# A residual block with split float32 matmuls: the distance between moving and stationary addresses is spread over 16 classes of 16 bytes

## The chip, the cores and the metric

The kernel runs on one core of one Trainium2 chip. The metric is the device time of one execution in microseconds, from runs of the same kernel; a profiled execution gives the trace beside it. TensorE (PE) does the matmuls, and its weight loads appear as an engine of their own (PEld), because they overlap the matmuls. VectorE is DVE, ScalarE is ACT, GpSimd is POOL, SyncE is SP.

## The reference, cut to what matters

One layer of a residual block over 512 tokens of width 2048 with 16 learned tokens in front. Three large products with float32 weights make up nearly all of the work:

```python
proj = h @ w_in                                   # 2048 x 12368
...                                               # sparse attention -> y_a, gated recurrence -> y_b
p = jnp.einsum('btnc,ncd->btnd', y, w_branch)     # 2 branches, 1024 x 2048 each
merged = jnp.sum(g * p, axis=2)
return x + merged @ w_out                         # 2048 x 2048
```

## The kernel before, in words

**Split products.** Each float32 operand is split into a high part, rounded to the type float32r, and the low rest. A product is then three matmuls: high by high, high weight by low moving, low weight by high moving (or, in the output, the same with the roles exchanged). The helper `hi_lo` (line 409) makes a tile `wh` (ScalarE, line 106) and a tile `wl` (VectorE, line 113; for 14 early tiles a ScalarE copy and a DMA that adds). `E.mm` records every matmul, at line 96 or 98.

**Pairs.** Most of `w_in` and all of `w_out` goes through a `Pair`: a two by two block product in the seven products of a Strassen-Winograd scheme. `SEVEN` lists them with their weights (`11`, `s2`, `12`, `s3`, `s1`, `22`, `s4`; an `s` is a sum of raw weight tiles), their moving operands and the PSUM bank that gathers them (`px`, `py`, `pz`, `pw`; `po` in the output). In `run_pair` one product is 8 blocks of 128 rows, and for each block three matmuls: `wh` by the high moving tile, `wh` by the low one, `wl` by the high one, 24 in all. The moving operands have 256 columns (tokens) in most pairs and 264 in those that need the 16 extra tokens as well. In `run_out` the roles are exchanged: the weight tiles are the moving operand of 256 columns and the tokens (`mh`) the stationary one. The weights of the next products are made two or three products ahead (`split_upto`).

**Single projections and branches.** A few column blocks of `w_in` (`kind == "in"`) and all of `w_branch` (`kind == "br"`) go through `split_chunk` and plain matmuls of 512 columns (`pg`), with 128 weight columns stationary and `hH`/`hL` or `yH`/`yL` moving.

**Where things lie.** The moving tiles live in 70 slots of 528 float32 each, 2112 bytes, which is 8 x 256 + 64. So slot number s starts at 64 x (s mod 4), counted modulo 256 bytes; the code calls s mod 4 the slot's home and asks `Slots.get` for a home when it makes such a tile (it takes another home if waiting for the right one would be long by its own clock). `HOME` gives for each of the seven products the home of the moving operand and which half of the tile it uses (the second half begins 264 x 4 = 1056 bytes on, that is 32 modulo 256); `YHOME` does so for the branches. The weight tiles have 1088 columns of which 1024 are used; all of them start at the same place modulo 256 bytes. `lead` (line 288) gives the column at which the 1024 used ones begin, 0 to 63, so it chooses the place of the weights modulo 256 bytes. Successive weight blocks inside a tile are 512 or 1024 bytes apart, so the place is the same for all of them.

**What `lead` does before.** It puts the weights so that moving address less stationary address is 192 modulo 256 bytes: `DIST` for the pairs and single projections, `DPO` for the output, `DBR` for the branches, all 192. One product of the seven cannot have it throughout: `22`, which uses `pw`, has the operand `t4`, whose high part is the first half of a slot of home 3 and whose low part is the second half of the same slot. There the high part is at 192 from the weights and the low part at 224. Where one product ends and the next begins, the distance is that of the old moving tile to the new weights.

**Order of work.** The instruction order on every engine is recorded by hand: tasks for attention, recurrence and index scores are slipped in between matmuls by a clock of estimated times (`pump`). Their matmuls appear as `phl`, `phd`, `psc` and others. Neither this clock nor the choice of slots reads a tile's offset.

Of the kernel before, what the change touches and what calls it, by code (L numbers as in the profile page):

```python
# [37 lines left out]
LAT = 180.0  # L38
SAME = {"pe": 0.0, "act": 60.0, "dve": 125.0, "pool": 60.0}
MARGIN = 300.0  # L40
DIST = 192
DPO = 192
DBR = 192
HOME = {"11": (0, 0), "s2": (2, 1), "12": (1, 0), "s3": (0, 1), "s1": (2, 0), "22": (3, 0), "s4": (1, 1)}
YHOME = (3, 0)
NSLOT = 70
# [152 lines left out]
def hybrid_kernel(ctx, tc, x, meta, vecs, w_in, rows, w_branch, w_out,  # L199
# [85 lines left out]
    def slot(name, dt=F32, home=None):  # L285
        return S.get(name, dt, home)

    def lead(home, byte, turn=False):
        return (64 * home + byte + (DPO if turn else -DIST)) % 256 // 4


    X = {}
# [101 lines left out]
    def load_upto(i):  # L394
        while state["dma"] <= min(i, len(stream) - 1):
            load_chunk(stream[state["dma"]])
            state["dma"] += 1

    def split_upto(i):
        while state["split"] <= min(i, len(preps_) - 1):  # L400
            k = state["split"]
            ch = preps_[k]
            if "pair" in ch:
                prep_op(k, ch)
            else:
                split_chunk(k, ch)
            state["split"] += 1

    def hi_lo(k, src, m, o):
        h, l = (wp.tile([128, 1088], F32R, name=f"w{i}{k}", tag=f"w{i}{k % NWS}")[:, o:o + 1024] for i in "hl")  # L410
        E.act(h[:, :m], src, AF.Copy)
        if 8 <= k < 22:
            n = l[:, :m]
            E.act(n, h[:, :m].bitcast(F32), AF.Copy, scale=-1.0)
            E.dma_add(n, src.bitcast(F32R))
        else:
            (E.ptt if k < 6 else E.tt)(l[:, :m], src, h[:, :m].bitcast(F32), OP.subtract)
        return h, l

    def split_chunk(k, ch):  # L420
        load_upto(ch["i"])
        m = ch["nk"] * ch["ncols"]
        r, nk, n = ch["raw"], ch["nk"], ch["ncols"]
        ch["h"], ch["l"] = [], []
        if k < 4:
            for g in range(2):
                h, l = slot("eh", F32R), slot("el", F32R)
                w = 4 * n
                E.act(h[:, :w], r[:, w * g:w * g + w], AF.Copy)
                (E.ptt if k > 1 else E.tt)(l[:, :w], r[:, w * g:w * g + w], h[:, :w].bitcast(F32), OP.subtract)  # L430
                early.extend((h, l))
                ch["h"] += [h[:, n * i:n * i + n] for i in range(4)]
                ch["l"] += [l[:, n * i:n * i + n] for i in range(4)]
        else:
            j = ch["job"]
            o = lead(YHOME[j.n], DIST - DBR) if j.kind == "br" else lead(ch["k0"] // 8, 32)
            h, l = hi_lo(k, r[:, :m], m, o)
            ch["h"] = [h[:, n * i:n * i + n] for i in range(nk)]
            ch["l"] = [l[:, n * i:n * i + n] for i in range(nk)]
        load_upto(ch["i"] + NRAW)  # L440
# [22 lines left out]
    def prep_op(k, op):  # L463

        pr, nm = op["pair"], op["name"]
        first = pr.raw["11"]["i"]
        load_upto(first + (0 if nm == "11" else 2 if nm == "s2" else 3))
        raw = {c: ch["raw"] for c, ch in pr.raw.items() if "raw" in ch}
        if nm in raw:
            src = raw[nm]  # L470
        else:
            for f in (sum_1, sum_2, sum_3, sum_4)[:int(nm[1]) if nm != "s1" else 1]:
                f(pr)
            src = {"s1": pr.s1, "s2": pr.s2, "s3": raw["21"], "s4": raw["12"]}[nm]
        home, half = HOME[nm]
        h, l = hi_lo(k, src, 1024, lead(home, 0, True) if pr.kind == "out" else
                     lead(home, 1056 * half + 4 * (264 - pr.w)))
        w = pr.ncols
        op["h"] = [h[:, w * i:w * i + w] for i in range(pr.nk)]
        op["l"] = [l[:, w * i:w * i + w] for i in range(pr.nk)]  # L480
        used = {"s3": 2, "22": 3, "s4": 4}.get(nm)
        if used:
            load_upto(first + used - 1 + NRAW)
# [1325 lines left out]
    for n in (1, 0):  # L1809
        for p in range(8):  # L1810
            for i in range(2):
                j = p + 8 * i
# [48 lines left out]
    for half in range(2):  # L1861
        n = (272, 256)[half]
        for kt in range(KT):
            prep_next()
            for ji in range(2):
                if ji == 0:
                    c = slice(272 * half, 272 * half + n)
                    o = kb[:80, half, :n]
                else:
                    c = slice(8 + 264 * half, 264 + 264 * half)  # L1870
                    o = qb[:, 256 * half:256 * half + 256]
# [148 lines left out]
```

## Time and profile before

| | |
|---|---|
| median of 2 runs | 1467.54 us (1467.2 to 1467.88) |
| the profiled execution | 1466.14 us |
| its span, first to last instruction | 1464.4 us |
| matmuls / weight loads | 12544 / 12544 |
| weight tiles made on VectorE (`wl`) | 289 from `raw`, 102 from `sum` |
| DMA | 263.26 MB, mean 180 GB/s |

Times in the profile are microseconds, those of one instruction in a group nanoseconds. A row of a group reads: line, engine, operation, outputs and inputs by the program's names, shapes, count, then busy time and mean duration of one, then the idle time of the engine ahead of them and what ended it. `128*128 128x256` on a matmul is weights of 128 by 128 and a moving operand of 256 columns. A piece of the chain reads: start, duration, engine, tile, line, count. A row of the timeline reads: start, duration, engine, line, operation, names, shape, count; matmuls overlap there, so the time from one start to the next is shorter than a duration. A row of the stretches reads: from and to, length, then the busy time and the count of PE, PEld, DVE, ACT and POOL, then the granted clock, the share of the DMA engines and GB/s.

### The profile page before, as it was taken

To read this page: it belongs to the slowest core of one execution; us is meant where nothing else is said; L and a number is where in the kernel's file an instruction comes from. 1 tells how busy PE (TensorE), PEld (TensorE's weight loads), DVE (VectorE), ACT (ScalarE), POOL (GpSimd) and SP (SyncE) were. 2 spreads that over 40 slices of the span, in tenths; PEclk is the share of its full clock that TensorE was granted. 3 is DMA by queue.
4 is the path that set the end of the run, shared out by engine and by line. 5 is a ranking of instruction groups with operands and counts; after the bars stand their busy time and mean duration, and the time that the engine had idled before them with its cause. 6 is when DMAs were issued, how large, how long until landed. Compare 5 with 4: busy or idle time off the path is not lost.

```text
span 1464.4 us, 31517 instructions
## 1 busy us (share of the span) xinstructions
PE 1448.0 (99%) x12544; PEld 1378.0 (94%) x12544; DVE 1183.1 (81%) x2017; ACT 715.7 (49%) x1172; POOL 272.5 (19%) x346
## 2 busy tenths in 40 slices
PE   7999999999999999999999999999999999999999
PEld 6888899999999999999999999999998888889998
DVE  6699799999999988878877887888776755878775
ACT  5576644544544554444444444444467752334332
POOL 2201000002233310100001011000365310102222
PEclk9999999999999999999999999999999999999999
DMA  9266677878889986768688687768895344458873
GB/s 278 74 157 140 154 181 190 191 183 202 204 207 227 251 197 165 176 164 199 161 202 182 152 204 177 176 162 193 208 283 160 101 125 142 144 137 223 214 214 92
DMA packets 336067, 263.26 MB, mean 180 GB/s; under 512 B 32484, under 2 KB 303408, under 8 KB 335920
## 3 DMA queue, kind: packets, MB, share of 16 engines
q1 hardware_dynamic: 306160, 174.51, 41.9%
q0 software_dynamic: 24256, 80.45, 28.3%
q10 hardware_dynamic: 5504, 6.29, 1.4%
q8 instruction: 99, 1.62, 0.4%
q14 instruction: 48, 0.39, 0.1%
HBM read 170.40 MB, written 29.98 MB: 137 GB/s over the span
## 4 chain that ended last, share of the span: by engine, by line
PE 93%; DVE 3%; DMA 2%; issue 1%; ACT 1%; POOL 0%; SPq 0%; DVEq 0%; POOLq 0%; ACTq 0%
PE pg L98 20%; PE px L96 16%; PE pz L96 15%; PE py L96 15%; PE po L96 11%; PE pw L96 8%; PE psc L98 1%; PE phl L98 1%; PE pov L96 1%; PE plg L98 1%; PE pho L98 1%; DVE wl L113 1%; PE ppt L102 1%; DMA raw<-raw 1%; PE px L102 1%
## 5 line engine op out<-in xcount | busy, mean ns | idle before, releaser
L106 ACT ACTIVATE wh<-raw 128x1024 fp32r<-128x1024 f32 x305 | 323.4, 1061 | 453.5 <-PE pz L96 116.5
L113 DVE TENSOR_TENSOR wl<-raw,wh 128x1024 fp32r<-128x1024 f32 x289 | 355.1, 1229 | 97.6 <-ACT wh L106 96.7
L96 PE MATMUL px<-hH,wh 128*128 128x256 f32 (+1 forms) x688 | 194.9, 283 | 0.0
L96 PE MATMUL px<-hH,wl 128*128 128x256 f32 (+1 forms) x688 | 192.6, 280 | 0.0
L96 PE MATMUL px<-hL,wh 128*128 128x256 f32 (+1 forms) x688 | 192.4, 280 | 0.0
L106 ACT ACTIVATE wh<-sum 128x1024 fp32r<-128x1024 f32 x102 | 108.3, 1062 | 154.5 <-PE pw L96 64.0
L98 PE MATMUL pg<-yH,wh 128*128 128x512 f32 x512 | 162.9, 399 | 1.0 <-DVE pTL L113 0.9
L96 PE MATMUL po<-wh,mh 128*128 128x256 f32 x896 | 156.6, 279 | 0.0
L113 DVE TENSOR_TENSOR wl<-sum,wh 128x1024 fp32r<-128x1024 f32 x102 | 129.6, 1271 | 27.0 <-ACT wh L106 26.6
L96 PEld LDWEIGHTS po<-wh,mh 128*128 128x128 f32 x896 | 136.9, 189 | 0.0
L96 PEld LDWEIGHTS px<-hH,wh 128*128 128x128 f32 x688 | 129.6, 188 | 0.6
L96 PEld LDWEIGHTS px<-hL,wh 128*128 128x128 f32 x688 | 129.6, 188 | 0.0
L96 PEld LDWEIGHTS px<-hH,wl 128*128 128x128 f32 x688 | 129.5, 188 | 0.0
L96 PE MATMUL pw<-tT,wh 128*128 128x256 f32 (+1 forms) x688 | 126.6, 284 | 1.5 <-DVE attn L1209 1.5
L96 PE MATMUL po<-wl,mh 128*128 128x256 f32 x448 | 125.1, 279 | 0.0
L96 PE MATMUL pz<-tT,wh 128*128 128x256 f32 (+1 forms) x688 | 122.9, 280 | 0.0
L96 PE MATMUL py<-tT,wh 128*128 128x256 f32 (+1 forms) x688 | 122.4, 279 | 0.0
L98 PEld LDWEIGHTS pg<-yH,wh 128*128 128x128 f32 x512 | 93.2, 188 | 21.3 <-PE pg L98 1.3
L96 PEld LDWEIGHTS pw<-tT,wh 128*128 128x128 f32 x688 | 105.4, 188 | 2.2 <-PE pz L96 2.0
L122 POOL DMA_DIRECT2D raw<-raw x51 | 44.3, 869 | 327.6 <-DVE sum L113 293.7
L96 PEld LDWEIGHTS py<-tT,wh 128*128 128x128 f32 x688 | 104.7, 188 | 0.0
L96 PEld LDWEIGHTS pz<-tT,wh 128*128 128x128 f32 x688 | 104.5, 188 | 0.1
(316 smaller groups left out, 3770.7 us busy)
## 6 DMA issues: line engine op xcount, KB each, us to landing
raw<-in_w_in_dram SPq DMA_DIRECT2D x192, 512.0 KB, 4.7
raw<-raw POOLq DMA_DIRECT2D x51, 512.0 KB, 5.3
raw<-sum POOLq DMA_DIRECT2D x51, 512.0 KB, 5.4
raw<-in_w_branch_dram SPq DMA_DIRECT2D x32, 512.0 KB, 4.7
raw<-in_w_out_dram SPq DMA_DIRECT2D x32, 512.0 KB, 4.2
gd<-g SPq DMA_DIRECT2D x32, 256.0 KB, 5.1
g<-gd POOLq DMA_DIRECT2D x30, 256.0 KB, 3.3
wl<-raw POOLq DMA_DIRECT2D x14, 512.0 KB, 4.5
```

The lines of the kernel that those rows point to most:

```text
L96: self.nc.tensor.matmul(out, lhsT, rhs, start=start, stop=stop, skip_group_check=True)
L98: self.nc.tensor.matmul(out, lhsT, rhs, start=start, stop=stop)
L102: self.nc.tensor.transpose(out, in_, ident)
L106: self.nc.scalar.activation(out, in_, f, **kw)
L113: self.nc.vector.tensor_tensor(out, a, b, op=op)
L122: self.nc.gpsimd.dma_start(out, a, accum_op=OP.add)
```

## The change

`lead` no longer uses one distance. It counts the weight tiles of each kind (`"in"`, `"br"`, `"out"`, and the pairs by their width 256 or 264) and gives the i-th of a kind the distance 16 x (7i + 3(i // 16)) modulo 256, so that 16 successive tiles take all 16 multiples of 16 bytes, in steps of 112, and the next 16 begin 48 bytes further. `wh` and `wl` of one tile share their distance. The sign for the output is the opposite, since there the weights are what moves. Nothing else is changed; the instructions of every engine are the same and stand in the same order.

```diff
-DIST = 192
-DPO = 192
-DBR = 192
+TURN = {}
...
-    def lead(home, byte, turn=False):
-        return (64 * home + byte + (DPO if turn else -DIST)) % 256 // 4
+    def lead(home, byte, kind):
+        i = TURN[kind] = TURN.get(kind, -1) + 1
+        dist = 16 * (7 * i + 3 * (i // 16)) % 256
+        return (64 * home + byte + (dist if kind == "out" else -dist)) % 256 // 4
...
-            o = lead(YHOME[j.n], DIST - DBR) if j.kind == "br" else lead(ch["k0"] // 8, 32)
+            o = lead(YHOME[j.n], 0, "br") if j.kind == "br" else lead(ch["k0"] // 8, 32, "in")
...
-        h, l = hi_lo(k, src, 1024, lead(home, 0, True) if pr.kind == "out" else
-                     lead(home, 1056 * half + 4 * (264 - pr.w)))
+        h, l = hi_lo(k, src, 1024, lead(home, 0, "out") if pr.kind == "out" else
+                     lead(home, 1056 * half + 4 * (264 - pr.w), pr.w))
```

## The prediction

> **What bounds the kernel now.** I read the engine table of the page first, then the chain that ended last, then the granted clock.
>
> ```profile
> PE 1448.0 (99%) x12544; PEld 1378.0 (94%) x12544; DVE 1183.1 (81%) x2017; ACT 715.7 (49%) x1172; POOL 272.5 (19%) x346
> PE 93%; DVE 3%; DMA 2%; issue 1%; ACT 1%; POOL 0%; SPq 0%; DVEq 0%; POOLq 0%; ACTq 0%
> core 0: 1464.4 us, clock 0.999
> ```
>
> TensorE is busy 99% of the span and makes 93% of the chain, at an undisturbed clock. The kernel is therefore as long as its matmuls stand apart, start to start; what another engine gains or loses matters only if it starves TensorE. The duration that a row gives a matmul (277 ns and the like) overlaps its neighbours and is no price. The price is the pace: a piece of the chain divided by its matmuls.
>
> The change moves no instruction: engine by engine, both built programs have the same instructions in the same order. Only addresses inside the weight tiles differ. So the question is whether the pace depends on where the moving operand of one matmul lies against the weights that are loaded beneath it. How many matmuls are concerned, by width, is in the groups of instructions with shapes kept apart and in two pieces of the chain:
>
> ```profile
> L96 PE MATMUL px<-hH,wh 128*128 128x256 f32 x496 | 139.4, 281 | 0.0
> L96 PE MATMUL px<-hH,wh 128*128 128x264 f32 x192 | 55.6, 289 | 0.0
> L98 PE MATMUL pg<-yH,wh 128*128 128x512 f32 x512 | 162.9, 399 | 1.0 <-DVE pTL L113 0.9
> L98 PE MATMUL pg<-hH,wh 128*128 128x512 f32 x144 | 57.1, 397 | 0.0
> 1207.92 96.48 PE pg L98 x417
> 1304.40 156.41 PE po L96 x1344
> 134.91 13.98 PE pg L98 x60
> ```
>
> A pair has seven products of 24 matmuls (8 weight blocks, 3 terms), and `px` with `hH,wh` holds 16 of the 168. So 496 / 16 = 31 pairs are 256 wide (31 x 168 = 5208 matmuls) and 192 / 16 = 12 pairs are 264 wide (2016). The output has 1344 of 256. The branch has 512 x 3/2 = 768 of 512 columns, the single projections 144 x 3 = 432.
>
> **The pace today, distance 192.** Pieces of the chain in one stretch of 256-wide pairs, and two from a later one:
>
> ```profile
> 600.38 2.73 PE py L96 x24
> 605.96 2.76 PE py L96 x24
> 608.72 2.73 PE pz L96 x24
> 618.19 2.74 PE px L96 x24
> 620.93 2.74 PE py L96 x24
> 627.28 2.82 PE py L96 x24
> 630.10 2.73 PE pz L96 x24
> ...
> 721.81 2.73 PE pz L96 x24
> 724.54 2.85 PE pw L96 x24
> ```
>
> Most products run 2.73 / 24 = 113.75 ns apart; one of the same form at the same distance took 2.82 / 24 = 117.5. The product `pw` takes 2.85 / 24 = 118.8. The seven first rows average 2.75 (114.6 ns); with one `pw` in seven the mean is (6 x 2.75 + 2.85) / 7 = 2.764 us, 115.2 ns.
>
> **`pw` is the one regular exception in the code, and so my key.** Its moving operand `t4` keeps its high half at byte 192 + 32 = 224 of the 256-byte class and its low half 1056 bytes on, at 0. The weights were placed for the high half only (224 - 32 = 192). So whenever the low half streams, the distance to the weights being loaded is 0 - 32 = 224. In order of time, against `pz`, whose halves agree:
>
> ```profile
> 721.65 0.39 PE L96 MATMUL pz<-tT,wh 128*128 128x256 f32 x2
> 721.88 0.28 PE L96 MATMUL pz<-tT,wl 128*128 128x256 f32 x1
> 721.99 0.39 PE L96 MATMUL pz<-tT,wh 128*128 128x256 f32 x2
> ...
> 724.38 0.40 PE L96 MATMUL pw<-tT,wh 128*128 128x256 f32 x2
> 724.62 0.28 PE L96 MATMUL pw<-tT,wl 128*128 128x256 f32 x1
> 724.74 0.40 PE L96 MATMUL pw<-tT,wh 128*128 128x256 f32 x2
> ```
>
> From the first start of a row of two to the `wl` row are two steps: 0.24 us in `pw`, 0.23 in `pz`; the third step is 0.12 against 0.11. A third of `pw`'s steps at 224 thus raises the whole triple by (2.85 - 2.73) / 8 = 15 ns. Address distance, or something that goes with it, moves the pace by some per cent.
>
> The 264-wide pairs behave otherwise. Undisturbed pieces, `pw` with its 224 among them, and a stretch just after other matmuls broke the stream:
>
> ```profile
> 655.41 2.91 PE pz L96 x24
> 658.32 2.89 PE pw L96 x24
> ...
> 691.36 0.29 PE L96 MATMUL px<-hL,wh 128*128 128x264 f32 x1
> 691.96 0.29 PE L96 MATMUL px<-hH,wh 128*128 128x264 f32 x1
> 692.09 0.30 PE L96 MATMUL px<-hL,wh 128*128 128x264 f32 x1
> 692.22 0.29 PE L96 MATMUL px<-hH,wl 128*128 128x264 f32 x1
> 692.47 0.28 PE L96 MATMUL px<-hL,wh 128*128 128x264 f32 x1
> 694.03 0.28 PE L96 MATMUL px<-hH,wl 128*128 128x264 f32 x1
> ```
>
> Here 224 costs nothing (2.89 / 24 = 120.4 ns). After the break, nine steps take 692.47 - 691.36 = 1.11 us, 123 ns each with single ones of 130; the next thirteen take 1.56 us, 120 each. The stream drifts through worse phases of moving against loading, then locks. Other distances may well lock in such places.
>
> **The change part by part.** It removes the common distance 192 and gives the n-th tile of a kind the distance 16 x (7n + 3(n // 16)) mod 256. All 16 classes come equally often, so 15/16 of the matmuls leave 192. In the built program, the pairs' matmuls indeed spread nearly evenly over the classes.
>
> *Pairs, 256 wide.* Lower bound of the price of leaving: none, or back to 113.75 (-1.45 ns). Upper bound: `pw`'s 15 ns put wholly on the one step at 224, 113.75 + 15 = 128.75. I take `pw`'s own mean, 118.8, since the second lock at 117.5 and the mixed steps of `pw` lie near it: (118.8 - 115.2) x 15/16 = 3.4 ns, x 5208 = +17.6 us.
>
> *Pairs, 264 wide.* Between 0 (`pw` above) and 123.3 - 120.0 = 3.3 ns. I take 1.5, in the middle: x 15/16 x 2016 = +2.8 us.
>
> *Output.* It stands at 156.41 / 1344 = 116.4 ns, between the two locks already. Bounds 113.75 and 128.75; I take 118.0, between the second lock and `pw`: 1.6 x 15/16 x 1344 = +2.0 us.
>
> *512 wide.* The projections, all at 192, run 13.98 / 60 = 233.0 ns apart. The branch runs 96.48 / 417 = 231.4, and in the built program some of its moving tiles fell into slots of other classes, so that it is a mixture of 0, 64 and 192 today. Other distances are no worse here: 432 x -1.6 x 15/16 = -0.6 us, nothing for the branch.
>
> *Writers.* The same ScalarE and VectorE instructions and DMAs fill the tiles, now from any 16-byte start. I cost that at nothing. VectorE is the nearest to a bound:
>
> ```profile
> 200.00:300.00 100.00, 100.00 (x870) 100.00 (x869) 96.64 (x196) 49.34 (x61) 8.48 (x10) 1.00 0.81 191
> L113 DVE TENSOR_TENSOR wl<-raw,wh 128x1024 fp32r<-128x1024 f32 x289 | 355.1, 1229 | 97.6 <-ACT wh L106 96.7
> L113 DVE TENSOR_TENSOR wl<-sum,wh 128x1024 fp32r<-128x1024 f32 x102 | 129.6, 1271 | 27.0 <-ACT wh L106 26.6
> wl<-raw POOLq DMA_DIRECT2D x14, 512.0 KB, 4.5
> ```
>
> The two split forms differ by 42 ns; even if each of the 391 lost that, it were 16 us of VectorE's time against 3.4 us idle in its fullest 100 us, where, at 391 over 1464 us, some 27 fall (1.1 us). Slower matmuls widen this cover. Without cover it would cost up to 16 us. The 14 DMAs land after 4.5 us and are asked three products (8.2 us) ahead.
>
> Sum: 17.6 + 2.8 + 2.0 - 0.6 = +21.8 us. On the profiled execution (1466.14 us, of which the span is 1464.4) that is 1487.9; that run lies 1.4 us under the median of 1467.54, so I forecast **1489.3 us** (+1.5%).
>
> **Rivals.**
> *Distance decides nothing.* What differs is the phase in which a product happens to start: `py` at 2.73 and 2.82 at one distance speaks for it, the regular `pw` against it. Time 1467.5.
> The Trainium skill, SBUF — State Buffer, section "Who interferes with whom", gives TensorE two independent read ports, one for the moving operand and one for the weights, and says that it waits on nobody; by that rule this rival is the outcome. The trace agrees for the 264-wide `pw` (120.4 ns) and not for the 256-wide one (118.8 against 113.75).
>
> *Bad classes.* A few distances lock in the worst phase, as 224 would at 128.75. With a quarter of the classes there and the rest at 118.8 the 256-wide mean is 121.3: (121.3 - 115.2) x 15/16 x 5208 = +29.8; the 264-wide at +3.3: +6.2; the output at 121.3: +6.2; -0.6. Together +41.6, time 1509. It decides from a pair mean near 120 ns on. For it: single 130 ns steps above; and half of the classes, the odd multiples of 16 bytes, appear nowhere in these weight products today. Against it: the stream left those steps by itself.
>
> *192 is a poor place.* Everything 256 wide settles at 113.75: pairs -1.45 x 5208 = -7.6, output -2.65 x 1344 = -3.6, -0.6 for 512; time 1455.7. For it: the 512-wide rows. Against it: 118.8 in `pw`.
>
> **How the numbers follow.** Forecast 0.49 (own range 1477 to 1497), no effect 0.22, bad classes 0.25, a poor 192 0.04. The range 1466 to 1514 holds nearly all of the first two and most of the third. Two per cent, 29.4 us, is about what a measurement of this kernel can tell from no change; above 1496.9 lie the bad classes and an edge of the forecast, 0.28; faster by as much needs more than any row offers, 0.02; within, 0.70.
>
> **What would show it.** Right: same instruction counts, PE still 99%; products of 24 spread between 2.72 and 2.95 us by class rather than clustered at 2.73; `po` near 158.5 us for 1344; branch pieces unchanged. Wrong upward: products at 3.0 us and more without another matmul inside. Wrong downward: the cluster at 2.73 stays. Wrong in kind: idle time of PE behind `wl` or `wh`.

## The result, and the profile after

The changed kernel took 1484.37 us (median of 2 runs, 1483.74 to 1485.0) against 1467.54 before: the ratio is 1.0114, with a 95% interval of 1.0093 to 1.0134. The forecast was 1489.3. The profiled execution took 1485.0 us, 18.9 more than that of before.

The engine table, the chain and the clock of the changed kernel:

```profile
PE 1465.3 (99%) x12544; PEld 1395.4 (94%) x12544; DVE 1185.9 (80%) x2017; ACT 715.5 (48%) x1172; POOL 272.5 (18%) x346
PE 91%; DVE 3%; DMA 2%; issue 2%; ACT 1%; POOL 1%; DVEq 0%; ACTq 0%; POOLq 0%
core 0: 1483.2 us, clock 1.000
```

All counts are those of before, and TensorE is still busy for 99% of a longer span at full clock. VectorE has 2.8 us more, ScalarE none. So no engine became the bound; the matmuls themselves stand further apart. Pieces of the chain in the same stretch of pairs, all 256 wide:

```profile
613.82 2.88 PE py L94 x24
616.70 2.92 PE pz L94 x24
623.63 2.85 PE pz L94 x24
626.48 2.83 PE px L94 x24
629.32 2.73 PE py L94 x24
635.72 2.85 PE py L94 x24
645.13 2.84 PE pz L94 x24
```

By the order of the tiles and the addresses of the built program, these seven have the distances 96, 208, 176, 80, 192, 160 and 240. The one at 192 still takes 2.73 us; the others take 2.83 to 2.92, which is 118 to 122 ns a matmul. The output and the 512-wide pieces:

```profile
134.97 13.96 PE pg L96 x60
1224.30 96.82 PE pg L96 x417
1321.12 158.55 PE po L94 x1344
```

The output went from 156.41 to 158.55 us. The 512-wide pieces moved by less than 0.4 us each.

Where a reader wants more than pieces show, every matmul's start can be laid beside the addresses that the built program gives its operands. The time from one start to the next, grouped by kind, gives this (sums hold everything up to the next start; means leave out steps that are more than a quarter longer than the median, where other work came between):

| kind | steps | sum before, us | sum after, us | difference | mean step before, ns | after |
|---|---|---|---|---|---|---|
| pairs, 256 wide | 5208 | 609.7 | 625.1 | +15.4 | 115.3 | 118.2 |
| pairs, 264 wide | 2016 | 249.0 | 250.0 | +1.1 | 121.1 | 121.6 |
| output, 256 wide | 1343 | 156.3 | 158.4 | +2.1 | 116.4 | 118.0 |
| single projections, 512 wide | 432 | 100.9 | 100.6 | -0.4 | 233.0 | 232.2 |
| branches, 512 wide | 768 | 182.1 | 182.5 | +0.3 | 231.7 | 232.1 |

And the 256-wide pairs of the changed kernel by distance between the moving operand and the weights that are loaded during the step:

```text
distance    0    16    32    48    64    80    96   112   128   144   160   176   192   208   224   240
mean ns  119.4 118.2 117.4 117.2 118.0 118.2 119.5 119.2 118.2 119.0 117.6 118.7 114.3 119.1 118.1 118.2
```

One class stands apart, and it is the one that all tiles had before. The fifteen others lie within 2.3 ns of each other, 118.4 in the mean. The weights' own place modulo 256 bytes, without the moving operand, does not explain it: in the kernel before, the products other than `22` have their weights at 0, 96, 128, 160, 192 and 224, all at distance 192, and their steps average 113.6 to 116.7 ns place by place; in the changed kernel, weights at these same six places but at other distances give 117.2 to 118.6.

### The profile page after: what moved, and what is told of

The parts are those of the page before. It is cut to its first block, busy times and chain, and to the rows that moved or that the text cites. A ratio compares the mean times of both kernels' runs of the same rounds, so it can differ in the third digit from the quotient of the medians.

```text
span 1483.2 us, 31517 instructions
## 1 busy us (share of the span) xinstructions
PE 1465.3 (99%) x12544; PEld 1395.4 (94%) x12544; DVE 1185.9 (80%) x2017; ACT 715.5 (48%) x1172; POOL 272.5 (18%) x346
## 4 chain that ended last, share of the span: by engine, by line
PE 91%; DVE 3%; DMA 2%; issue 2%; ACT 1%; POOL 1%; DVEq 0%; ACTq 0%; POOLq 0%
PE pg L96 20%; PE px L94 15%; PE pz L94 15%; PE py L94 14%; PE po L94 11%; PE pw L94 7%; PE psc L96 1%; PE phl L96 1%; PE pov L94 1%; PE pho L96 1%; PE plg L96 1%; DVE wl L111 1%; PE ppt L100 1%; DMA raw<-sum 1%; DMA vr<-vd 1%
## 5 line engine op out<-in xcount | busy, mean ns | idle before, releaser
L104 ACT ACTIVATE wh<-raw 128x1024 fp32r<-128x1024 f32 x305 | 323.2, 1060 | 470.6 <-PE pz L94 118.5
L94 PE MATMUL pz<-tT,wh 128*128 128x256 f32 (+1 forms) x688 | 126.3, 284 | 0.0
```

Source lines behind the costliest of these rows:

```text
L94: self.nc.tensor.matmul(out, lhsT, rhs, start=start, stop=stop, skip_group_check=True)
L104: self.nc.scalar.activation(out, in_, f, **kw)
```

## The experiments

The theory after the result: each distance has a pace at which a 256-wide product settles, 192 has a much better one than nearly all others, and leaving it costs some 4 ns a matmul. Rivals: it is the change from tile to tile that costs (theory B); the phase in which a product starts decides, not the distance (C). And within the theory: does the weight tile count that is loaded during the matmul (N), the matmul's own (O), or both (J)? Except for the last experiment, a run is one execution, beside the kernel before on the same chip. Twelve executions of the kernel before spread from 1465.34 to 1469.04 us, so a difference of 2 us between single executions decides nothing by itself; the sums by kind do more, since kinds that an experiment leaves alone repeat within 1 us. Two diffs of the scans and the one of the run without the 256-wide pairs are against the changed kernel, the others against the kernel before; line numbers follow the one or the other.

**One common distance that is not 192.**

```diff
-DIST = 192
-DPO = 192
-DBR = 192
+DIST = 96
+DPO = 96
+DBR = 96
```

> All weight tiles at one distance, 96, instead of 192. Theory A (the distance itself sets the pace at which a product settles): in the changed kernel the undisturbed 256-wide products at 96 ran 119.8 ns apart, the 264-wide 123.1, the output 119.8, so pairs of 256 grow by (119.7 - 115.3) x 5208 = 23 us, of 264 by 4, the output by 4.6, the 512-wide by about 1: near 1499 us. Theory B (what costs is that neighbouring tiles have different distances, so that the stream must settle anew for each): one common distance costs little, 1467 to 1473 us. Theory C (no distance counts, only how a product starts): 1467.5 us.

It took 1498.58 us, beside 1467.15 for the kernel before. Pieces of its chain:

```profile
613.89 2.87 PE py L96 x24
622.60 2.88 PE pz L96 x24
```

```profile
134.73 13.90 PE pg L98 x60
1332.46 160.80 PE po L96 x1344
```

No product falls back to 2.73 although no tile differs from its neighbour: theory B is out, and so is C, since the same products in the same order are all slower. By kind, the 256-wide pairs grew by 20.7 us (119.5 ns a step), the 264-wide by 6.4, the output by 4.4. The class means of the changed kernel had given 1499, so this class keeps its pace when all tiles have it.

**The change without the 256-wide pairs.**

```diff
-        dist = 16 * (7 * i + 3 * (i // 16)) % 256
+        dist = 192 if kind == 256 else 16 * (7 * i + 3 * (i // 16)) % 256
```

> The change without its largest term: the 256-wide pairs stay at 192, all other tiles turn through the 16 classes. If the terms add, what is left is what the trace of the changed kernel shows outside the 256-wide pairs: output +2.1, 264-wide +1.1, 512-wide 0, so 1470.7 us, and the 256-wide pairs keep 609.7 us. If turning tiles disturb their neighbours too (a rival: the first products after a change of distance settle badly), the 256-wide pairs lose some us of their own and the time is above 1474.

It took 1468.86 us, 1.7 more than the run beside it and 2.7 more than the profiled execution of before. Two pieces:

```profile
608.65 2.73 PE pz L94 x24
1304.98 158.55 PE po L94 x1344
```

The pairs are back (610.1 us in all, against 609.7), and the output is where the change put it, 158.55. The terms add: 15.4 us of the 18.9 belong to the 256-wide pairs.

**How fine the good place is.** The 16 classes were put 4 bytes apart around 192, and then, for the 256-wide pairs alone, all 64 classes of 4 bytes were scanned:

```diff
-        dist = 16 * (7 * i + 3 * (i // 16)) % 256
+        dist = 160 + 4 * ((7 * i + 3 * (i // 16)) % 16)
```

> The distances take 16 classes of 4 bytes, 160 to 220, around 192, where the changed kernel took 16 of 16 bytes. If the pace goes by 16-byte lines, the four classes 192 to 204 (or 180 to 192) run alike near 114 ns in the 256-wide pairs and the twelve others at 117 to 119: pairs of 256 at about 117.3, time near 1480 us. If only 192 exactly is good, fifteen of sixteen classes run at 117.5 to 119 and the time is near 1484 us. If a place between the lines is better than 192, its class shows under 113.5.

```diff
-        dist = 16 * (7 * i + 3 * (i // 16)) % 256
+        dist = 4 * (27 * i + 5 * (i // 64)) % 256 if kind == 256 else 192
```

> The tiles of the 256-wide pairs turn through all 64 distances of 4 bytes, everything else stays at 192. In the last scan 180, 192 and 204 settled at 113.3 to 114 ns and nothing between them did. Theory L (the pace goes by 4-byte columns and has a good place every 12 bytes only near 192): the other classes give 116.5 to 122, three good of 64, mean near 118.3, time about 1483 us. Theory P (good places return every 12 bytes all around): some 21 of 64 classes settle under 115 and the mean falls to about 117, 1476 us.

They took 1485.0 us and 1480.91 us (beside 1467.15 and 1468.21). The first scan turned the output too, which lost 4.0 us of its own, so its time, near the 1484 of "only 192", does not tell the theories apart; the paces by distance do. Mean step of the undisturbed products, `pw` among them at the distance of its high half; the second scan has one to four such products for each distance:

```text
distance            160   164   168   172   176   180   184   188   192   196   200   204   208   212   216   220
first scan, ns     117.9 118.3 117.1 119.3 118.4 114.5 118.5 118.2 115.8 119.3 117.5 115.0 120.1 118.2 118.6 119.7
scan of 64, ns     117.5 118.4 114.0 119.3 118.6 115.2 118.2 118.0 115.1 119.7 117.9 114.6 117.9 118.0 119.0 119.8
```

The 48 other distances of the second scan lie between 116.8 and 120.6. Good places come every 12 bytes, at 180, 192 and 204 and (in one scan) 168, and no other class has so low a mean; the lowest single product elsewhere, at 248, averaged 115.9, while the other one there, a `pw`, took 117.9. Four bytes to either side of each good place the mean is back at 117.5 or more. The 115.8 at 192 holds two `pw` at 118.9; without them it is 115.0. The pace does not go by 16-byte lines. The change's steps of 16 bytes could meet only one of these places. The second scan's mean over all steps, 118.3, is what theory L said; its time lies nearer to L's 1483 than to P's 1476.

**Which weights count.** The low weight tile of each of the six products other than `22` was moved 96 bytes on; then the high one instead:

```diff
-        h, l = (wp.tile([128, 1088], F32R, name=f"w{i}{k}", tag=f"w{i}{k % NWS}")[:, o:o + 1024] for i in "hl")
+        h, l = (wp.tile([128, 1088], F32R, name=f"w{i}{k}", tag=f"w{i}{k % NWS}")[:, p:p + 1024]
+                for i, p in (("h", o), ("l", (o + more) % 64)))
...
-                     lead(home, 1056 * half + 4 * (264 - pr.w)))
+                     lead(home, 1056 * half + 4 * (264 - pr.w)), 24 * (nm != "22" and pr.kind == "pair" and pr.w == 256))
```

and in the second kernel, with the rest alike:

```diff
+                for i, p in (("h", (o + more) % 64), ("l", o)))
```

> As before, but in the six other products of the 256-wide pairs the low weight tile lies 96 bytes further on: the high tile stays at 192 from the moving operands, the low one goes to 96. In a triple (high weights by high moving, high weights by low moving, low weights by high moving) the first step then has 192 against its own weights and against those being loaded; the second has 192 against its own and 96 against those being loaded; the third has 96 against its own and 192 against those being loaded. Theory N (the weights being loaded count): the second step rises from 114 to near 119, the others stay; pairs of 256 +7 us, 1474. Theory O (its own weights count): the third step rises, the others stay; +7 us, 1474. Theory J (both loads lie under a matmul in turn, so that one wrong neighbour already spoils the resonance of all steps): all three steps rise to 116 to 119; +13 to +18 us, 1480 to 1485.

> The mirror of the run with the low weights moved: here the high weight tile goes to 96 and the low one stays at 192, in the same six products. Loading distance now is 96 in the first and third step and 192 in the second; own distance is 96 in the first and second and 192 in the third. If loading counts most and the own weights little (7 and 2 ns, as the other run gave): third step near 122, first near 120, second near 117; pairs of 256 +18 to +22 us, time 1486 to 1490 us. If own weights counted as much, the second step would be as slow as the third.

They took 1481.4 us (beside 1468.21) and 1482.31 us (beside 1467.67, the median of 12). The mean of each step of a triple, in ns, by the distance of the moving operand to its own weights and to those being loaded, from the starts and addresses:

| step | low moved: own, loaded | ns | high moved: own, loaded | ns |
|---|---|---|---|---|
| high by high | 192, 192 | 115.9 | 96, 96 | 119.1 |
| high by low | 192, 96 | 121.9 | 96, 192 | 116.1 |
| low by high | 96, 192 | 116.8 | 192, 96 | 119.4 |

Of the two mixed cases, the one with 96 to the loaded weights costs 121.9 and 119.4, the one with 96 to its own 116.8 and 116.1. In the kernel before, the three steps run alike, at 114.5, 114.7 and 114.4 ns, so the differences do not come from a step's place in the triple. By the steps, theory N has the larger part: what matters first is where the moving operand lies against the weights that are loaded beneath it. By the times, neither N nor O came: they said 1474 for the first kernel, and 1481.4 is in the range of J. All three steps rose, and in neither kernel does one get back to the pace of before. The second kernel was expected at 1486 to 1490 and took 1482.31, because all three steps came lower than expected: 119.1, 116.1 and 119.4 instead of 120, 117 and 122. So one wrong neighbour slows all steps, and the step that has it at its loaded weights most. Pieces of whole products show it; none is at 2.73, of the first kernel and then of the second:

```profile
626.42 2.84 PE px L96 x24
629.25 2.84 PE py L96 x24
```

```profile
625.74 2.82 PE px L96 x24
628.57 2.82 PE py L96 x24
```

**The exception of the old kernel.** In product `22` only the low weight tile was moved, by 32 bytes, so that the low half of `t4` meets its loaded weights at 192. `hi_lo` is as in the first of the two kernels above:

```diff
+                     lead(home, 1056 * half + 4 * (264 - pr.w)), 8 * (nm == "22" and pr.kind == "pair"))
```

> As before, but the low weight tile of product 22 (bank pw) lies 32 bytes further, so that the low half of t4 is 192 from the weights that are loaded while it streams. Theory N (what counts is the moving operand against the weights that are loaded under it, those of the next matmul): all three steps of a triple are then at 192 and the 256-wide pw falls from 118.8 to about 114 ns: 744 x 4.8 = 3.6 us less, near 1464 us. Theory O (the moving operand against its own weights counts): the third step moves to 160 and the second stays at 224, pw stays at 118 or more, 1467.5 us. The 264-wide pw (120.4) changes by under 1 us under either.

It took 1467.98 us, beside 1467.15; the 1464 of theory N did not come. The product in order of time:

```profile
725.30 0.40 PE L96 MATMUL pw<-tT,wh 128*128 128x256 f32 x2
725.54 0.28 PE L96 MATMUL pw<-tT,wl 128*128 128x256 f32 x1
725.66 0.40 PE L96 MATMUL pw<-tT,wh 128*128 128x256 f32 x2
...
727.32 0.28 PE L96 MATMUL pw<-tT,wl 128*128 128x256 f32 x1
```

A triple still takes 0.36 us. All three steps load weights at 192 and run at 119.4, 119.4 and 117.6 ns, where before they ran at 118.8, 122.0 and 115.4. So 192 to the loaded weights is not enough. What this product keeps is a moving operand that alternates between two places 32 bytes apart, and in two of three steps a distance of 224 or 160 to its own weights. Which of these holds it back wasn't separated.

**Another of the good places, for all.**

```diff
-                     lead(home, 1056 * half + 4 * (264 - pr.w)))
+                     lead(home, 1056 * half + 4 * (264 - pr.w), dist=180 if pr.w == 256 else DIST))
```

Here and in the next experiment `lead` takes the distance as an argument `dist`, which is `DIST` unless it is given.

> As before, but the 256-wide pairs stand at 180 instead of 192. In the fine scan all twelve undisturbed products at 180 settled at 113.3 ns and averaged 114.5, also those in bank py with hH, which at 192 mostly stay at 117.7; undisturbed products at 192 averaged 115.0. If a class keeps its pace when all tiles have it, the pairs lose about 2 us and the time is near 1465 us; pw stands at 180 and 212 and is the unknown (plus or minus 1 us). If the scan's 180 was good only because it stood among other distances: 1467 us or more.

It took 1469.32 us, beside 1468.21: a miss of the expected 2 us of gain. Three products `s3`, `s2` and `s4`, in this order:

```profile
627.95 2.74 PE py L96 x24
621.59 2.76 PE py L96 x24
637.14 2.88 PE pz L96 x24
```

`s3`, which took 2.82 at this point before, takes 2.74, as the scan said. But `s2` rose from 2.74 to 2.76, single products such as the `pz` at 637.14 settled at 2.88, and `pw` rose from 118.8 to 119.3 ns. The mean step of all 256-wide pairs is 115.3, as before; 180 is a place as good as 192, not a better one. The scan's advantage for `s3` was real (all 25 undisturbed ones now settle at 113, where 18 of 25 kept 118 before), but it was eaten up elsewhere.

**A distance for each kind.** The scans named faster places for other shapes, and for two products.

```diff
-            o = lead(YHOME[j.n], DIST - DBR) if j.kind == "br" else lead(ch["k0"] // 8, 32)
+            o = lead(YHOME[j.n], 0, dist=16) if j.kind == "br" else lead(ch["k0"] // 8, 32, dist=172)
...
-                     lead(home, 1056 * half + 4 * (264 - pr.w)))
+                     lead(home, 1056 * half + 4 * (264 - pr.w),
+                          dist={"s3": 180, "22": 224}.get(nm, DIST) if pr.w == 256 else DIST))
```

> As before, but each kind takes the distance at which the earlier traces show it settle fastest: 172 for the 512-wide single projections (227.4 ns in the fine scan against 233.0), 16 for the branches (229.8 against 231.7), 180 for product s3 (bank py with hH, 114.5 against 116.7) and 224 for product 22 (bank pw, 117.7 against 118.8) in the 256-wide pairs; the rest stays at 192. If the classes keep their pace: -2.4 -0.6 -1.6 -0.8 = -5.4 us, near 1462 us. If a product's pace depends as much on how the one before it ended (the trial with all pairs at 180 gave back on five products what it won on one): the 512-wide gain stays and the pairs' part is between -2 and +2 us, 1462 to 1467 us.

It took 1463.56 us (median of 8 executions) against 1467.67 (median of 12): a ratio of 0.997, interval 0.9959 to 0.998. It is faster than both kernels, than the one before by only 0.3%. Two rows of the single projections, 54 matmuls apart:

```profile
134.27 0.40 PE L98 MATMUL pg<-hH,wh 128*128 128x512 f32 x1
...
146.56 0.39 PE L98 MATMUL pg<-hH,wh 128*128 128x512 f32 x1
```

They run 12.29 / 54 = 227.6 ns apart, where at 192 it was 233.0. By kind the 512-wide projections gained 1.8 us and the branches 0.9, near the expected 2.4 and 0.6. The pairs' mean step fell from 115.3 to 114.9 ns, but five more of their steps became long, and their sum did not fall in the profiled execution. That one, 1465.43 us, was the slowest of the eight, so the trace shows 2.7 of the 4.1 us gained, and where the rest lies is not shown.

## Why the prediction was right, point by point

- **What bounds.** Right. The matmuls' pace sets the time; the counts and the busy share of PE did not change, and no wait for `wh` or `wl` appeared.
- **256-wide pairs, +17.6.** It was +15.4. The present pace was read as 115.2 ns and is 115.3; the price of leaving was taken from `pw`, 118.8, and the other classes average 118.4; times 15/16 that is 2.9 ns a matmul instead of 3.4.
- **Output, +2.0.** It was +2.1 (158.55 us; "near 158.5" was said). The 118.0 ns was chosen between two paces of the pairs, 117.5 and 118.8, so that it fits to a tenth is in part luck.
- **264-wide pairs, +2.8.** It was +1.1. The middle between 0 and 3.3 ns was too high; the row of `pw` at 224, which cost nothing, was the better guide. In the experiment with one distance 96 this width lost 6.4 us, so it has bad classes; in the changed kernel seven of the fifteen others averaged less than its 121.4 ns at 192 and eight more.
- **512-wide, -0.6.** It was -0.1: -0.4 for the projections, +0.3 for the branches.
- **Writers, 0.** Right. The rows of the changed kernel, VectorE's splits and the adding DMAs, are those of before within 5 ns and 0.1 us; in the DMA's row the last number is the time to landing in us:

```profile
L111 DVE TENSOR_TENSOR wl<-raw,wh 128x1024 fp32r<-128x1024 f32 x289 | 356.3, 1234 | 107.0 <-ACT wh L104 105.1
L111 DVE TENSOR_TENSOR wl<-sum,wh 128x1024 fp32r<-128x1024 f32 x102 | 129.9, 1274 | 28.6 <-ACT wh L104 28.1
wl<-raw POOLq DMA_DIRECT2D x14, 512.0 KB, 4.5
```

- **Sum.** +21.8 was forecast and +18.9 came between the profiled executions (+16.8 between the medians); the 256-wide term was 2.2 us too large and the 264-wide one 1.7, the 512-wide one 0.5 too small, and some tenths lie elsewhere.
- **The rivals.** "Distance decides nothing" is refuted by the run at 96. That was also what the Trainium skill gives (SBUF — State Buffer, section "Who interferes with whom": independent ports, TensorE waits on nobody); the measured pace of the 256-wide products, 113.3 to 120 ns by nothing but the address of the weights, does not agree. "Bad classes" did not come: the odd multiples of 16 bytes average 118.5 and the even ones without 192 average 118.3. "192 is a poor place" holds for 512 columns alone: in the projections 172 gains 5 ns, and in the branches 16 in place of the old mixture gains about 1.
- **The key was half right.** `pw` gave the right price, but not for the reason stated. The prediction put its excess down to the third of its steps that is at 224. In the changed kernel, with its high half at 224 and its low half at 0, `pw` ran at 117.7, faster than at 192 and 224; and with every loaded weight at 192 it stayed at 119. Before the change its steps at 192 were slow too (118.8 and 115.4 ns beside 122.0 at 224), so its excess is not the price of one distance. Why it is slow stays open, and that its 118.8 lay so near the 118.4 of the other classes was in part luck; the second support of the price, the pace of 117.5 that one product at 192 kept, lay near it too.

## What to carry to other kernels

In this kernel's matmuls with 256 moving columns of float32r, run back to back, the place of the weights against the moving operand, modulo 256 bytes, is worth 3 to 5% of the pace, and good places are rare and as narrow as one 4-byte column. In a kernel of this kind, set it on purpose for each shape, and scan it in one execution by giving successive tiles successive distances, as this change does. What such a scan shows of a class held when all tiles were given it at 96 (to 1 us in 31), but the 2 us that were expected of 180 did not come: a product's pace also depends on how the one before it ended. And a price may be right though its cause is not: test the cause on the one product that has it.

## What the runs showed of the hardware that was not expected

- The fast distances for 256 moving columns lie 12 bytes apart (180, 192, 204, and 168 in one scan), and the scan of 64, thin as it is, found no other class as fast; the settled step there (the mean of a product's second half) is 113.3 to 114 ns, at nearly all others 116.7 to 120. Why 12 bytes, and why there, stays open.
- The effect depends on the width. With 264 columns, 176, 192, 208 and 224 alike settle near 120 ns, while at 96 products settled at 121.6 or 126; with 512 columns 172 gives 227.6 ns and 192 gives 233.0.
- By the second half of its 24 steps a product keeps one of a few paces; at 192 these are 113.3 to 114 and 117.7, and which one it takes depends on how the product before ended. The 25 undisturbed products `s3` of the kernel before show it: all 18 whose predecessor ended on steps of 113 to 114 ns (the very last apart) stay near 117.7, and all 7 whose predecessor ended on steps of 117 to 119 settle at 113.3. So at one distance the start decides between two paces, as theory C has it; between 192 and 96 it does not.
